# MLP up products of four groups as seven block products, with weight sums made in DRAM by timed DMAs

## The chip, the cores and the metric

The kernel runs on one core of a Trainium2 chip. The metric is the device time of one execution in microseconds (us); the time of a kernel is the median of its runs. Five engines each work through their own list of instructions: TensorE (PE) multiplies, VectorE (DVE), ScalarE (ACT) and GpSimd (POOL) do the elementwise work, SyncE (SP) issues transfers (DMAs). POOL issues transfers too. Semaphores order one engine's work behind another's.

## The reference

One layer on a sequence of 512 frames with 1024 features: a mixer (forgetting attention beside a gated recurrence), cross attention to 256 memory frames, and an MLP, each added to the residual, then a last norm. The change lies in the MLP (d_ff is 4096):

```python
u = rmsnorm(h, norm_ff_g[l]) @ w1[l]
h = h + jnp.square(jax.nn.relu(u)) @ w2[l]
return rmsnorm(h, final_norm_g)
```

All is float32. The kernel splits each operand into a high and a low part and computes a product as three matmuls: high by high, high by low, low by high.

## The kernel before, in words

The program is written out by hand; each engine works in program order, apart from places where a filler (`fill`) puts projections between the steps of the attention. Up to about 430 us it does the mixer and the cross attention. Weights come through SP in pieces of 512 KB into raw tiles (`wr`), ACT makes the high part (`wh`, L175) and DVE the low part (`wl`, L179).

The MLP works in eight groups of 512 hidden features. **Up**: for each of two halves `j` of the group and each of two blocks `i` of 128 features, a PSUM bank `u` takes 8 x 3 matmuls of 512 columns (`mlp_up`, `gemm_fm`, L240 to L242; weights stationary, x moving as `x_hi` and `x_lo`). ACT makes the squared ReLU in two steps (`square`, L1306 and L1307). **Down**: each group's product is a 2 by 2 block product (rows of frames by halves of features) in seven products instead of eight, after Strassen and Winograd (`mlp_down`, `PLAN`): `hidden_sums` combines the hidden blocks, `hidden_part` splits a combination into `hb`, and seven combined weight blocks are multiplied with them in banks U, V and Y. DVE adds a bank to the accumulator `acc` after the products that complete it, scaled by the norm's factor `rsq` (`add_to`, L1334). Up of group g+1 comes before down of group g; the last two groups' downs are done together, and `last_product` ends the program.

The combined weight blocks of the down are made in the SBUF: SP loads five raw blocks of w2 per group into eight slots (`load_raws`, tiles `wq`), and four accumulating transfers, issued by POOL (`add_weights`, L1244), add one block to another: two from DRAM (`first_adds`), two from slot to slot. The up's units are `wru`, `whu`, `wlu`; the down's `wq`, `whd`, `wld`. `unit` keeps four split units ahead of PE.

In the mixer, the biases of the forgetting attention (`bi`, L926 and L927) are made on POOL, for pairs of heads and one to four blocks of 128 keys, and DVE adds them to the scores (L946).

Of the kernel before, what the change touches and what calls it, by code (L numbers as in the profile page):

```python
# [38 lines left out]
NEG = -3.0e38  # L39


@with_exitstack
def emit(
# [189 lines left out]
    def gemm_fm(ps, wt, col, ahi, alo, n=S, order=range(KC), begun=False):  # L233

        whi, wlo = wt
        sl = slice(col, col + P)
        for n_, k in enumerate(order):
            hi, lo = chunk(ahi, k, slice(0, n)), chunk(alo, k, slice(0, n))
            wh, wl = chunk(whi, k, sl), chunk(wlo, k, sl)
            te.matmul(ps, wh, hi, start=n_ == 0 and not begun, stop=False)  # L240
            te.matmul(ps, wh, lo, start=False, stop=False)  # L241
            te.matmul(ps, wl, hi, start=False, stop=k == order[-1])  # L242
            yield 3 * n / 2400

    def gemm_tm(ps, wt, ahi, alo, tb, nk=KC):
# [3 lines left out]
        for k in range(nk):  # L249
# [5 lines left out]
            te.matmul(ps, lo, wh, start=False, stop=k == nk - 1)  # L255
            yield 3 * n / 2400

    def gemm_wide(pss, ahi, alo, done):

        for half in range(2):  # L260
            whi, wlo = next_panel()
            for u in range(2):
                for tb, ps in enumerate(pss):
                    sl = slice(tb * P, (tb + 1) * P)
                    for kk in range(2):
# [4 lines left out]
                        te.matmul(ps, lo, whi[u][:, kk, :], start=False, stop=k == KC - 1)  # L270
                        yield 3 * S / 2400
# [127 lines left out]
    xTd = drp.tile([4, P, 2, S], F32, name="xTd")  # L399
    park = {}  # L400
# [817 lines left out]
    slots = [t[:, i, :] for t in [ap_.tile([P, 4, D], F32, tag="act", name=f"wq{j}") for j in range(2)] for i in range(4)]  # L1218
    HS = S // 2
    units, raws, unit_q = {}, {}, deque()  # L1220
    sqs, comb, hbs = {}, {}, {}

    def up_units(g):
        for j in range(2):
            spec = panel(w1, g * HG + j * WT)
            for n in range(2):

                def prep(g=g, j=j, n=n, spec=spec):
                    if (j, n) == (0, 0):
                        down_raws(g - 1)  # L1230
                    unit, splits = load_unit(f"u{g}{j}{n}", spec, slice(n * UK, (n + 1) * UK))
                    with ahead(PW):
                        for split in splits:
                            split()
                    units["u", g, j, n] = unit

                unit_q.append((("u", g, j, n), prep))

    quad = {"a1": (0, 0), "c1": (0, 0), "a2": (0, 1), "b2": (1, 1), "b1": (1, 0)}
    PRODUCTS = ("1", "2", "6", "5", "7", "3", "4")  # L1240

    def add_weights(raw, src):

        gp.dma_start(raw.rearrange("p (k n) -> p k n", k=2), src, accum_op=ALU.add)  # L1244

    RAWS = ("a1", "c1", "a2", "b2", "b1")

    def load_raws(g, names):
        w = raws.setdefault(g, {})
        for name in names:  # L1250
            r, c = quad[name]
            n = 5 * g + RAWS.index(name)
            w[name] = slots[n % 8] if n < 38 else k4([D], f"wq{n}")
            src = w2[g * HG + r * 2 * P : g * HG + (r + 1) * 2 * P, c * S : (c + 1) * S].rearrange("(k p) n -> p k n", p=P)
            nc.sync.dma_start(w[name].rearrange("p (k n) -> p k n", k=2), src)
            w[name, "src"] = src

    def first_adds(g):
        w = raws[g]
        add_weights(w["a2"], w["b2", "src"])  # L1260
        add_weights(w["c1"], w["a2", "src"])

    def down_raws(g):

        load_raws(g, RAWS)
        first_adds(g)


    RAW = {"1": "a1", "2": "b1", "5": "c1", "3": "b2", "6": "a1", "7": "a2", "4": "b1"}

    def down_units(gs):
        def prep(g, name):
            w = raws[g]
            raw = w[RAW[name]]
            unit = new_parts([2, S], f"d{g}{name}")
            with ahead(PW):
                split_of(unit[0], unit[1], raw.rearrange("p (k n) -> p k n", k=2))()
            if name == "2":
                for to, of in (("a1", "a2"), ("b1", "a1")):
                    add_weights(w[to], w[of].rearrange("p (k n) -> p k n", k=2))  # L1280
            units["d", g, name] = unit

        for name in PRODUCTS:
            for g in gs:
                unit_q.append((("d", g, name), lambda g=g, name=name: prep(g, name)))
# [9 lines left out]

    def mlp_up(g, j, wt):
        for i in range(2):
            ps = mm(f"u{g}{j}{i}")
            run_now(gemm_fm(ps, wt, i * P, x2_hi, x2_lo))
            yield g, j, i, ps  # L1300

    def square(g, j, i, ps):
        if i == 0:
            sqs[g, j] = k4([2, S], f"sq{g}{j}")
        u = sqs[g, j][:, i, :]
        ac.activation(u, ps, AF.Relu)  # L1306
        ac.activation(u, u, AF.Square)  # L1307

    def hidden_sums(g):
# [7 lines left out]
        comb[g] = {"1": A1a, "5": s5, "6": n6, "3": s3, "7": s7, "2": A1b, "4": A2b}  # L1317

# [11 lines left out]

    def add_to(ps, rows, half, t, sign):
        tb = 2 * rows + t
        a = acc[tb][:, half * S : (half + 1) * S]
        ve.scalar_tensor_tensor(a, ps, rsq[sign][:, tb : tb + 1], a, op0=ALU.mult, op1=ALU.add)  # L1334


    PLAN = {
        "1": ("U", True, ((0, 0, 1),)),
# [4 lines left out]
        "2": ("V", True, ((0, 0, 1),)),  # L1343
# [3 lines left out]
    def mlp_down(gs):  # L1347
# [3 lines left out]
        for n, name in enumerate(PRODUCTS):  # L1351
# [4 lines left out]
            for g, t in [(g, t) for g in gs for t in range(2)]:  # L1356
                whi, wlo = unit("d", g, name)
                hb = hbs[g, name]
                if first_ and g == gs[0]:
                    banks[bank, t] = {"U": sc, "Y": tr, "V": mm}[bank](f"{bank}{g}{t}")  # L1360
# [193 lines left out]
```

## Time and profile before

| | us |
|---|---|
| Three runs | 766.42, 766.53, 766.06 |
| Median | 766.42 |
| Profiled execution | 766.06 |
| Its span (first to last instruction) | 764.3 |
| PE busy | 755.3 |
| DVE busy | 502.8 |
| ACT busy | 388.6 |
| POOL busy | 170.3 |

The span holds everything that the profile shows; 1.7 us of the execution lie outside it. Busy times of different engines overlap. A row of matmuls gives how long one is in flight, and several are at once: the pace is the distance between start times. A row of a transfer gives the time from its issue to its landing. A row of a group reads: line, engine, operation, output and input, count, then busy time and the mean in ns, then the idle time of the engine ahead of it and what ended that.

### The profile page before, as it was taken

The page shows a single profiled execution, that of the slowest core. Times are in us where ns is not written, and L with a number is a line of the kernel's source. Part 1 is how long each engine was busy: PE and PEld are TensorE (multiplying, and loading weights), DVE is VectorE, ACT ScalarE, POOL GpSimd, SP SyncE. Part 2 cuts the span into 40 slices and gives each one's busy share as a digit, 9 for nine tenths or more (in the row PEclk, how much of TensorE's full clock was granted, in tenths as well). Part 3 has the DMA queues.
Part 4 walks back from the last instruction along what each step waited for, and adds up shares of the span by engine and source line. Part 5 has one row for each costly group of instructions (what it writes and reads, how often), then busy time and mean ns, then how long its engine had stood idle before and what let it go on. Part 6 is the DMA issues. An engine that isn't in the chain of part 4 may idle for free.

```text
span 764.3 us, 10886 instructions
## 1 busy us (share of the span) xinstructions
PE 755.3 (99%) x4069; PEld 635.5 (83%) x4069; DVE 502.8 (66%) x816; ACT 388.6 (51%) x657; POOL 170.3 (22%) x248
## 2 busy tenths in 40 slices
PE   9999999999999999999999999999999999999996
PEld 6889888888889988888888888888888888888885
DVE  5647863678877656555546445939495776767596
ACT  6655554656666523344444456455454545353653
POOL 7207531322542225310000110101001010101123
PEclk9999999999999999999999999999999999999999
DMA  8652333313635432222113595575758575758602
GB/s 241 201 138 58 85 84 111 111 56 111 197 111 172 138 129 83 84 98 67 56 56 103 204 280 129 153 171 160 179 156 198 143 189 142 193 138 217 141 1 110
DMA packets 78870, 103.01 MB, mean 135 GB/s; under 512 B 4657, under 2 KB 56410, under 8 KB 78818
## 3 DMA queue, kind: packets, MB, share of 16 engines
q1 hardware_dynamic: 69266, 76.61, 32.1%
q0 software_dynamic: 8960, 24.67, 15.5%
q10 hardware_dynamic: 592, 1.05, 0.4%
q8 instruction: 32, 0.52, 0.3%
q14 instruction: 20, 0.16, 0.1%
HBM read 89.71 MB, written 4.21 MB: 123 GB/s over the span
## 4 chain that ended last, share of the span: by engine, by line
PE 95%; DVE 2%; ACT 1%; POOL 1%; issue 1%; ACTq 0%; POOLq 0%
PE u L240 8%; PE u L241 8%; PE u L242 8%; PE U L1366 4%; PE U L1367 4%; PE U L1368 4%; PE xq L240 2%; PE wo L240 2%; PE xq L241 2%; PE xq L242 2%; PE xw L241 2%; PE xw L242 2%; PE wo L242 2%; PE xw L240 2%; PE wo L241 2%; PE Y L1366 2%
## 5 line engine op out<-in xcount | busy, mean ns | idle before, releaser
L179 DVE TENSOR_TENSOR wld<-wq,whd 128x1024 fp32r<-128x1024 f32 x56 | 68.8, 1240 | 46.8 <-ACT whd L175 46.8
L240 PE MATMUL u<-x_hi,whu 128*128 128x512 f32 x192 | 74.7, 389 | 0.0
L241 PE MATMUL u<-x_lo,whu 128*128 128x512 f32 x192 | 74.7, 389 | 0.0
L242 PE MATMUL u<-x_hi,wlu 128*128 128x512 f32 x192 | 74.7, 389 | 0.0
L175 ACT ACTIVATE whd<-wq 128x1024 fp32r<-128x1024 f32 x56 | 58.3, 1052 | 29.7 <-PE u L241 18.5
L1244 POOL DMA_DIRECT2D wq<-in_w_dram x16 | 19.4, 1228 | 178.4 <-DMA wq<-in_w_dram 124.7
L175 ACT ACTIVATE whu<-wru 128x1024 fp32r<-128x1024 f32 x24 | 25.3, 1053 | 56.9 <-DMA wru<-in_w_dram 56.9
L179 DVE TENSOR_TENSOR wlu<-wru,whu 128x1024 fp32r<-128x1024 f32 x24 | 29.3, 1222 | 33.0 <-ACT whu L175 33.0
L1366 PE MATMUL U<-whd,hb 128*128 128x512 f32 x120 | 46.7, 389 | 0.0
L1367 PE MATMUL U<-wld,hb 128*128 128x512 f32 x120 | 46.7, 389 | 0.0
L1368 PE MATMUL U<-whd,hb 128*128 128x512 f32 x120 | 46.7, 389 | 0.0
L242 PEld LDWEIGHTS u<-x_hi,wlu 128*128 128x128 f32 x192 | 36.0, 188 | 7.5
L240 PEld LDWEIGHTS u<-x_hi,whu 128*128 128x128 f32 x192 | 36.0, 188 | 7.5
L241 PEld LDWEIGHTS u<-x_lo,whu 128*128 128x128 f32 x192 | 36.0, 188 | 7.4
L1244 POOL DMA_DIRECT2D wq<-wq x16 | 14.1, 880 | 125.0 <-DVE wld L179 95.6
L1334 DVE SCALAR_TENSOR_TENSOR acc<-U,rsq,acc 128x512 f32<-128x512 f32 x56 | 39.8, 744 | 0.3 <-PE U L1393 0.3
L926 POOL TENSOR_SCALAR bi<-nF,Ft 128x128 f32<-128x128 f32 (+3 forms) x32 | 23.0, 726 | 58.0 <-PE pt L958 37.0
L1306 ACT ACTIVATE sq<-u 128x512 f32<-128x512 f32 x32 | 18.7, 584 | 20.5 <-PE u L242 20.5
L1368 PEld LDWEIGHTS U<-whd,hb 128*128 128x128 f32 x120 | 22.5, 188 | 4.7
L1366 PEld LDWEIGHTS U<-whd,hb 128*128 128x128 f32 x120 | 22.5, 188 | 4.7
L1367 PEld LDWEIGHTS U<-wld,hb 128*128 128x128 f32 x120 | 22.5, 188 | 4.7
L1324 ACT ACTIVATE hb<-s 128x512 fp32r<-128x512 f32 x24 | 15.0, 629 | 20.6 <-PE U L1368 13.6
(957 smaller groups left out, 2262.1 us busy)
## 6 DMA issues: line engine op xcount, KB each, us to landing
wq<-in_w_dram SPq DMA_DIRECT2D x40, 512.0 KB, 3.4
wru<-in_w_dram SPq DMA_DIRECT2D x24, 512.0 KB, 6.4
wq<-in_w_dram POOLq DMA_DIRECT2D x16, 512.0 KB, 8.7
wq<-wq POOLq DMA_DIRECT2D x16, 512.0 KB, 4.9
xTd<-xT POOLq DMA_DIRECT2D x4, 512.0 KB, 4.1
nF<-Fd POOLq DMA_DIRECT2D x8, 256.0 KB, 3.9
hT<-xTd POOLq DMA_DIRECT2D x4, 512.0 KB, 5.3
xt<-in_x_dram SPq DMA_DIRECT2D x3, 512.0 KB
```

The lines of the kernel that those rows point to most:

```text
L175: ac.activation(hi, raw, AF.Copy)
L179: ve.tensor_tensor(lo, raw, f(hi), ALU.subtract)
L240: te.matmul(ps, wh, hi, start=n_ == 0 and not begun, stop=False)
L241: te.matmul(ps, wh, lo, start=False, stop=False)
L242: te.matmul(ps, wl, hi, start=False, stop=k == order[-1])
L926: gp.tensor_scalar(bi[:, 0:n], fF[h][:, 0:n], -1.0, Ft[:, tb, h : h + 1], op0=ALU.mult, op1=ALU.add)
L1244: gp.dma_start(raw.rearrange("p (k n) -> p k n", k=2), src, accum_op=ALU.add)
L1306: ac.activation(u, ps, AF.Relu)
L1334: ve.scalar_tensor_tensor(a, ps, rsq[sign][:, tb : tb + 1], a, op0=ALU.mult, op1=ALU.add)
L1366: te.matmul(ps, hi, whi[:, k, :], start=begin, stop=False, skip_group_check=True)
L1367: te.matmul(ps, hi, wlo[:, k, :], start=False, stop=False, skip_group_check=True)
L1368: te.matmul(ps, lo, whi[:, k, :], start=False, stop=k == 1, skip_group_check=True)
```

## The change

**Up.** For groups 4 to 7 (`SEVEN`) the up is a block product in seven products too (`mlp_up7`). The four quarters of a group's weights (512 inputs by 256 features) and of x (512 inputs by 256 frames) are combined; each product has 4 x 2 x 3 matmuls of 256 columns. The combinations of x are made once, during the up of group 1 (`x_sums`). Products go to three banks: "1" to U, "5" to Y, "6" adds to U, "2" goes to V, "7" adds to U, "3" to Y, "4" to U. ACT copies U to V after "1" and to Y after "6", and Y after "5" to the tile `y5`, which DVE adds to two results (the sign is turned in the square's step).

**Weight sums.** For each group's down, and for the ups of groups 4 to 7, the four combined weight blocks are made in DRAM (`sum_jobs`, tiles `wsd` and `wsu`): eight transfers each, four copies (L427) and four accumulates (L425), all issued by POOL. A class `Presum` counts matmul time (2400 columns a us) as the program is written; after 80 us, and then after each 5 us, the next transfer is made to wait for the matmul just written. Jobs alternate in pairs. SP then loads raw and combined blocks alike (L1290) into a ring of five raw tiles. The accumulates and the slots in the SBUF go; the slots' room holds the combinations of x.

**Down.** The products' order becomes "1", "5", "6", "2", "7", "3", "4". "1" isn't added to `acc` any more: ACT copies its U into V (L1489), where "2" adds to it, so DVE does 12 adds a group, not 14. `acc` is scaled once by mean square + eps before the first down, so the adds need no factor, and the last norm's eps is scaled alike (`eps3`). `hidden_ahead` makes the hidden parts up to four products ahead.

The diff, cut:

```diff
+SEVEN = (4, 5, 6, 7)
+RAWS, HB = 5, 4
+PRE0, PRE = 80.0, 5.0
...
-            te.matmul(ps, wl, hi, start=False, stop=k == order[-1])
-            yield 3 * n / 2400
+            at = te.matmul(ps, wl, hi, start=False, stop=k == order[-1])
+            yield presum.tick(3 * n / 2400, at)
...
+    SUMS = {"5": ("00", "01"), "7": ("01", "11"), "6": ("5", "11"), "4": ("6", "10")}
+
+    def block1(g, rc):
+        r, c = int(rc[0]), int(rc[1])
+        n0 = g * HG + c * WT
+        return w1[r * S : (r + 1) * S, n0 : n0 + WT].rearrange("(k p) n -> p k n", p=P)
+
+    def block2(g, rc):
+        r, c = int(rc[0]), int(rc[1])
+        k0 = g * HG + r * 2 * P
+        return w2[k0 : k0 + 2 * P, c * S : (c + 1) * S].rearrange("(k p) n -> p k n", p=P)
+
+    wsum = {}
+
+    def sum_jobs(kind, g):
+        block, shape = (block1, [P, UK, WT]) if kind == "u" else (block2, [P, 2, S])
+        for name in SUMS:
+            wsum[kind, g, name] = drp.tile(shape, F32, name=f"ws{kind}{g}{name}")
+        for name, add in (("5", 0), ("7", 0), ("5", 1), ("7", 1), ("6", 0), ("6", 1), ("4", 0), ("4", 1)):
+            dst, (a, b) = wsum[kind, g, name], SUMS[name]
+            if add:
+                yield gp.dma_start(dst, block(g, b), accum_op=ALU.add)
+            else:
+                yield gp.dma_start(dst, wsum[kind, g, a] if a in SUMS else block(g, a))
+
+    class Presum:
+        def __init__(self):
+            self.jobs, self.left = deque(), PRE0
+
+        def tick(self, us, at):
+            self.left -= us
+            while self.left <= 0.0 and self.jobs:
+                job = self.jobs[0]
+                dma = next(job, None)
+                if dma is None:
+                    self.jobs.popleft()
+                    continue
+                sync = mybir.DependencyInfo(mybir.DependencyClass.Sync, mybir.DependencyReason.DATA)
+                tc.add_manual_dep(dma.ins, at.ins.name, sync, reason="presum")
+                if len(self.jobs) > 1:
+                    self.jobs[0], self.jobs[1] = self.jobs[1], self.jobs[0]
+                self.left += PRE
+            return us
+
+    presum = Presum()
+    for g in range(DFF // HG):
+        presum.jobs.append(sum_jobs("d", g))
+        if g + 2 in SEVEN:
+            presum.jobs.append(sum_jobs("u", g + 2))
...
+    PRODUCTS = ("1", "5", "6", "2", "7", "3", "4")
+    QUAD = {"1": "00", "2": "10", "3": "11"}
+    raw_n = [0]
+
+    def raw_tile(name):
+        raw_n[0] += 1
+        if raw_n[0] % RAWS in (0, 2):
+            return wrp.tile([P, D], F32, tag="wr", name=f"wr{name}", padded_shape=[P, UK * UW])
+        return s4([D], f"wr{name}")
+
+    def add_unit(key, shape, src):
+
+        def prep():
+            name = "".join(map(str, key))
+            unit = new_parts(shape, name)
+            raw = raw_tile(name).rearrange("p (k n) -> p k n", k=shape[0])
+            nc.sync.dma_start(raw, src())
+            with ahead(PW):
+                split_of(unit[0], unit[1], raw)()
+            units[key] = unit
+
+        unit_q.append((key, prep))
 
     def up_units(g):
+        if g in SEVEN:
+            for name in PRODUCTS:
+                add_unit(("u", g, name), [UK, WT], lambda name=name: block1(g, QUAD[name]) if name in QUAD else wsum["u", g, name])
+            return
         for j in range(2):
...
+                add_unit(("d", g, name), [2, S], lambda g=g, name=name: block2(g, QUAD[name]) if name in QUAD else wsum["d", g, name])
...
+    def mlp_up7(g):
+
+        qa, qb = (k4([2, S], f"sq{g}{j}") for j in range(2))
+        sqs[g, 0], sqs[g, 1] = qa, qb
+        h1, h2 = slice(0, HS), slice(HS, S)
+        bank = {}
+
+        for name in PRODUCTS:
+            b = {"5": "Y", "3": "Y", "2": "V"}.get(name, "U")
+            if b not in bank:
+                bank[b] = (pvt if b == "Y" else mm)(f"u{b}{g}").rearrange("p (i n) -> p i n", i=2)
+                if b == "V":
+                    pass
+            ps = bank[b]
+            whi, wlo = unit("u", g, name)
+            xh, xl = xsum[name]
+            for k in range(UK):
+                for i in range(2):
+                    ws, begin = slice(i * P, (i + 1) * P), name in "15" and k == 0 and i == 0
+                    te.matmul(ps[:, i, :], whi[:, k, ws], xh[:, k, :], start=begin, stop=False, skip_group_check=True)
+                    te.matmul(ps[:, i, :], whi[:, k, ws], xl[:, k, :], start=False, stop=False, skip_group_check=True)
+                    at = te.matmul(ps[:, i, :], wlo[:, k, ws], xh[:, k, :], start=False, stop=k == UK - 1, skip_group_check=True)
+                presum.tick(6 * HS / 2400, at)
+            if name == "1":
+                bank["V"] = mm(f"uV{g}").rearrange("p (i n) -> p i n", i=2)
+                ac.activation(bank["V"], ps, AF.Copy)
+            elif name == "5":
+                y5 = t2(f"y5{g}", F32, (2, HS))
+                ac.activation(y5, ps, AF.Copy)
+            elif name == "6":
+                ac.activation(bank["Y"], ps, AF.Copy)
+            elif name == "2":
+                square(ps, qa[:, :, h1])
+            elif name == "7":
+                ve.tensor_tensor(qb[:, :, h2], ps, y5, ALU.add)
+                square(qb[:, :, h2], qb[:, :, h2], -1.0)
+            elif name == "3":
+                ve.tensor_tensor(qb[:, :, h1], ps, y5, ALU.add)
+                square(qb[:, :, h1], qb[:, :, h1], -1.0)
+            else:
+                square(ps, qa[:, :, h2])
+            yield
...
+        for n, (a, b, sign) in (("5", ("4", "2a", -1)), ("6", (None, "1", 1)), ("3", (None, "2", -1)), ("7", ("1", "2a", -1))):
+            op = ALU.add if sign > 0 else ALU.subtract
+            if a is None:
+                ve.tensor_tensor(d, d, f(x_[b][0]), op)
+            else:
+                ve.tensor_tensor(d, f(x_[a][0]), f(x_[b][0]), op)
+                ve.tensor_tensor(d, d, f(x_[a][1]), ALU.add)
+            ve.tensor_tensor(d, d, f(x_[b][1]), op)
+            yield
+            hi, lo = out_[n]
+            ac.activation(hi, d, AF.Copy, scale=-1.0 if n == "6" else 1.0)
+            if n == "6":
+                ve.scalar_tensor_tensor(lo, d, -1.0, f(hi), op0=ALU.mult, op1=ALU.subtract)
+            else:
+                ve.tensor_tensor(lo, d, f(hi), ALU.subtract)
+            xsum[n] = (hi, lo)
+            yield
 
     def hidden_sums(g):
...
+    def hidden_ahead(key, n):
+
+        used = hb_order.index(key)
+        for k in hb_order[used : used + n]:
+            if k not in hbs and k[0] in comb:
+                hidden_part(*k)
...
-        ve.scalar_tensor_tensor(a, ps, rsq[sign][:, tb : tb + 1], a, op0=ALU.mult, op1=ALU.add)
-
+        a = acc[2 * rows + t][:, half * S : (half + 1) * S]
+        if sign > 0:
+            ve.tensor_tensor(a, ps, a, ALU.add)
+        else:
+            ve.scalar_tensor_tensor(a, ps, -1.0, a, op0=ALU.mult, op1=ALU.add)
...
             for g, t in [(g, t) for g in gs for t in range(2)]:
                 whi, wlo = unit("d", g, name)
+                hidden_ahead((g, name), 1)
...
-                if end and (g, t) == (gs[0], 1) and 1 <= n < len(PRODUCTS) - 1:
-                    hidden_part(NG - 1, PRODUCTS[n + 1])
-                for rows, half, sign in goes if g == gs[-1] else ():
+                    at = te.matmul(ps, lo, whi[:, k, :], start=False, stop=k == 1, skip_group_check=True)
+                presum.tick(6 * S / 2400, at)
+                if end and (g, t) == (gs[0], 1):
+                    hidden_ahead((g, name), HB + 1)
+                if g != gs[-1]:
+                    continue
+                if name == "1":
+                    banks["V", t] = mm(f"V{g}{t}")
+                    ac.activation(banks["V", t], ps, AF.Copy)
+                for rows, half, sign in goes:
                     add_to(ps, rows, half, t, sign)
                     if end and (name, rows) in FINAL:
                         finish(2 * rows + t, half)
-            if not end:
-                hidden_part(gs[0] + 1, name)
-            elif n == 0:
-                hidden_part(NG - 1, PRODUCTS[1])
+            hidden_ahead((gs[-1], name), HB)
+            yield
 
     def last_product(gs, banks):
...
+    e2 = cp.tile([P, NT], F32, name="e2")
+    eps3 = cp.tile([P, NT], F32, name="eps3")
...
+    gp.tensor_tensor(eps3, e2, e2, op=ALU.mult)
+    gp.tensor_scalar(eps3, eps3, EPS, 0.0, op0=ALU.mult, op1=ALU.add)
+    for tb in range(NT):
+        ac.activation(acc[tb], acc[tb], AF.Copy, scale=e2[:, tb : tb + 1])
```

**What moves on the engines.** First PE, in the fifth up (group 4). Before, a bank `u` ends after 24 matmuls of 512 columns, and the bank of the next 128 features begins, with the same weights unit:

```order
2854 L241 MATMUL u_5592<-x_lo,whu_5536 128x512
2855 L242 MATMUL u_5592<-x_hi,wlu_5537 128x512
2856 L240 MATMUL u_5620<-x_hi,whu_5513 128x512
2857 L241 MATMUL u_5620<-x_lo,whu_5513 128x512
2858 L242 MATMUL u_5620<-x_hi,wlu_5514 128x512
2859 L240 MATMUL u_5620<-x_hi,whu_5513 128x512
```

After, product "1" ends after 24 matmuls of 256 columns and "5" begins in the bank Y, with the combined x (`xs`):

```order
2854 L1353 MATMUL uU_5716<-x_lo,whu_5643 128x256
2855 L1354 MATMUL uU_5716<-x_hi,wlu_5644 128x256
2856 L1352 MATMUL uY_5749<-xs_hi,whu_5667 128x256 [waits Activation_49]
2857 L1353 MATMUL uY_5749<-xs_lo,whu_5667 128x256
2858 L1354 MATMUL uY_5749<-xs_hi,wlu_5668 128x256 [waits DVE_49]
2859 L1352 MATMUL uY_5749<-xs_hi,whu_5667 128x256
```

The number of matmuls until here is the same; a group's up takes 168 of 256 columns and not 96 of 512. Next ACT in the same up, before: two steps of a square for each bank, and splits of later units between them:

```order
463 L1306 ACTIVATE sq_5617<-u_5592 128x512 [waits PE_49]
464 L1307 ACTIVATE sq_5617<-sq_5617 128x512 [waits Activation_49]
465 L175 ACTIVATE whu_5582<-wru_5584 128x1024 [waits DMAHW1_49,DVE_49]
466 L175 ACTIVATE whd_5588<-wq_4461 128x1024 [waits DMAHW4_49,DVE_49,PE_49]
467 L175 ACTIVATE whd_5647<-wq_4460 128x1024 [waits DMAHW4_49,DVE_49,PE_49]
468 L1306 ACTIVATE sq_5617<-u_5620 128x512 [waits PE_49]
469 L1307 ACTIVATE sq_5617<-sq_5617 128x512 [waits Activation_49]
470 L1324 ACTIVATE hb_5740<-sq_5617 128x512 [waits Activation_49]
471 L1306 ACTIVATE sq_5682<-u_5657 128x512 [waits PE_49]
472 L1307 ACTIVATE sq_5682<-sq_5682 128x512 [waits Activation_49]
```

After, from the last split ahead of the copy of U into V:

```order
474 L178 ACTIVATE whu_5750<-wru_5752 128x1024 [waits DMAHW0_49,PE_49]
475 L1358 ACTIVATE uV_5747<-uU_5716 128x512 [waits PE_49]
476 L178 ACTIVATE whu_5783<-wru_5785 128x1024 [waits DMAHW1_49,PE_49]
477 L1361 ACTIVATE y_5781<-uY_5749 128x512 [waits PE_49]
478 L178 ACTIVATE whu_5814<-wru_5816 128x1024 [waits DMAHW2_49,DVE_49,PE_49]
479 L1363 ACTIVATE uY_5749<-uU_5716 128x512 [waits PE_49,Activation_49]
480 L1428 ACTIVATE hb_6004<-s_3_5537 128x512 [waits DVE_49]
481 L178 ACTIVATE whd_5847<-wrd_5849 128x1024 [waits DMAHW4_49,PE_49]
482 L1321 ACTIVATE sq_5714<-uV_5747 128x2x256 [waits PE_49]
483 L1322 ACTIVATE sq_5714<-sq_5714 128x2x256 [waits Activation_49]
```

Each copy that clears a bank stands behind one split; the squares come behind the third copy. Last POOL, in the mixer, where the biases for three blocks of keys (128x384) are made. Before:

```order
102 L926 TENSOR_SCALAR bi_1859<-nF_1583,Ft 128x384 [waits PE_49,Activation_49]
103 L926 TENSOR_SCALAR bi_1864<-nF_1585,Ft 128x384 [waits PE_49]
104 L927 AFFINE_SELECT bi_1859<-bi_1859 128x128 [waits Pool_49]
105 L927 AFFINE_SELECT bi_1864<-bi_1864 128x128 [waits Pool_49]
106 L926 TENSOR_SCALAR bi_1951<-nF_1583,Ft 128x512 [waits DVE_49,PE_49]
107 L926 TENSOR_SCALAR bi_1956<-nF_1585,Ft 128x512 [waits DVE_49,PE_49]
108 L927 AFFINE_SELECT bi_1951<-bi_1951 128x128 [waits Pool_49]
109 L927 AFFINE_SELECT bi_1956<-bi_1956 128x128 [waits Pool_49]
```

After:

```order
108 L425 DMA wsd_1266<-in_w_dram 256x1x512 [waits DMASW1_49,DMASW0_49,PE_49]
109 L425 DMA wsd_1311<-in_w_dram 256x1x512 [waits DMASW3_49,PE_49]
110 L979 TENSOR_SCALAR bi_1875<-nF_1596,Ft 128x384 [waits Activation_49]
111 L979 TENSOR_SCALAR bi_1880<-nF_1598,Ft 128x384
112 L980 AFFINE_SELECT bi_1875<-bi_1875 128x128 [waits Pool_49]
113 L980 AFFINE_SELECT bi_1880<-bi_1880 128x128 [waits Pool_49]
114 L427 DMA wsd_1267<-wsd_1265 16x8192 [waits DMASW6_49,DMASW2_49,PE_49]
115 L979 TENSOR_SCALAR bi_1968<-nF_1596,Ft 128x512 [waits DVE_49,PE_49]
116 L979 TENSOR_SCALAR bi_1973<-nF_1598,Ft 128x512 [waits DVE_49,PE_49]
117 L980 AFFINE_SELECT bi_1968<-bi_1968 128x128 [waits Pool_49]
```

Two accumulates that wait for a matmul (`PE`) now stand ahead of these biases, and a copy that waits for another ahead of the next.

158 lines of the change are left out of this document (62 added, 96 removed).

## The prediction

> **What bounds the kernel now.** I read the page first: the span, the busy times and the chain.
>
> ```profile
> span 764.3 us, 10886 instructions
> PE 755.3 (99%) x4069; PEld 635.5 (83%) x4069; DVE 502.8 (66%) x816; ACT 388.6 (51%) x657; POOL 170.3 (22%) x248
> PE 95%; DVE 2%; ACT 1%; POOL 1%; issue 1%; ACTq 0%; POOLq 0%
> ```
>
> PE is busy for 755.3 of 764.3 us, and 95% of the chain is its own. So two things only can move the end: less matmul time, or a wait of PE that is not there today. The view of waits, for PE, shows how little of the second there is:
>
> ```profile
> PE warm L352 <- DVE ones L356: 1.3, 1, 1.3
> PE pt L958 <- DVE bi L950: 0.7, 1, 0.7
> ```
>
> That is 2.0 us in the program and none of it in the MLP, which is where most of the change lies. The busy time by stages, for one up (first row) and one down product (second row) of the MLP, shows how far the others are from their limit there (columns: window, its length, then busy of PE, PEld, DVE, ACT, POOL with counts, the granted clock, the DMA engines' share, GB/s):
>
> ```profile
> 492.90:514.60 21.70, 21.70 (x98) 17.96 (x97) 11.13 (x13) 9.18 (x12) 2.97 (x3) 1.00 0.75 174
> 514.60:533.70 19.10, 19.10 (x86) 15.83 (x85) 17.66 (x24) 10.73 (x14) 1.21 (x1) 1.00 0.55 162
> ```
>
> PE fills both windows at the full clock. DVE is at 92% of the down window (17.66 of 19.10) and half idle in the up window; the DMA engines are at 0.75 and 0.55. These are the covers that the change spends.
>
> **The change part by part. 1. Matmuls.** An up group has 2 x 2 x 8 x 3 = 96 matmuls of 512 columns. Seven products on quarter blocks are 7 x 4 x 2 x 3 = 168 matmuls of 256 columns. The pace of each is read from the start times of matmuls that follow each other: 14 steps of the up product, and 21 steps of the memory keys' product, which has the same form as the new ones (weights stationary, 256 columns moving, x as hi and lo).
>
> ```profile
> 499.79 0.39 PE L242 MATMUL u<-x_hi,wlu 128*128 128x512 f32 x1
> ...
> 502.96 0.39 PE L241 MATMUL u<-x_lo,whu 128*128 128x512 f32 x1
> ```
> ```profile
> 246.33 0.28 PE L240 MATMUL xk<-meh,wh19a 128*128 128x256 f32 x1
> ...
> 248.85 0.28 PE L240 MATMUL xk<-meh,wh19a 128*128 128x256 f32 x1
> ```
>
> 3.17/14 = 0.2264 us and 2.52/21 = 0.120 us: half the columns cost 53%, not 50%. A group falls from 96 x 0.2264 = 21.7 us to 168 x 0.120 = 20.2 us: 1.6 us (21.73 less 20.16), and 6.3 us over four groups. One eighth of the products is saved, 2.7 us, and two fifths of that goes to the shorter matmuls' dearer columns. The down products keep their 84 matmuls.
>
> The Trainium skill, "TensorE: Matmul & The Clock Gate", section "Back-to-back issue gap", gives the isolated gap as N/2.4 + 2.5 ns, by which I estimate 109 and 216 ns, a gain of 2.4 us a group and of 9.5 us in all. The measured 120 and 226 ns are longer than both; the sum goes by them.
>
> **2. DMA.** This decides whether the gain arrives. Prices come from the page's queue table and the landing times of its issues:
>
> ```profile
> q1 hardware_dynamic: 69266, 76.61, 32.1%
> q0 software_dynamic: 8960, 24.67, 15.5%
> wq<-in_w_dram SPq DMA_DIRECT2D x40, 512.0 KB, 3.4
> wru<-in_w_dram SPq DMA_DIRECT2D x24, 512.0 KB, 6.4
> wq<-in_w_dram POOLq DMA_DIRECT2D x16, 512.0 KB, 8.7
> wq<-wq POOLq DMA_DIRECT2D x16, 512.0 KB, 4.9
> xTd<-xT POOLq DMA_DIRECT2D x4, 512.0 KB, 4.1
> nF<-Fd POOLq DMA_DIRECT2D x8, 256.0 KB, 3.9
> hT<-xTd POOLq DMA_DIRECT2D x4, 512.0 KB, 5.3
> ```
>
> q1 takes 0.321 x 764.3 = 245 us of all 16 engines for 76.61 MB, so a load of 512 KB (0.524 MB) takes 1.68 us. q0 takes 118.5 us; its plain transfers (xTd, hT, nF, and mt and gfin, 7.9 MB) at q1's rate take 25.3 us, which leaves 93.2 us for 32 accumulates, 2.91 us each. These prices give the stage rows back: an up and a down hold 9 loads and 4 accumulates, 9 x 1.68 + 4 x 2.91 = 26.8 us, and the rows say 0.75 x 21.7 + 0.55 x 19.1 = 26.8.
>
> After the change, an up and a down of groups 4 to 7 last 20.2 + 19.0 = 39.2 us and need 14 loads, seven a stage, 23.5 us. The sums in DRAM come every 5 us of matmul time, counted at 2400 columns a us (168 x 256 + 84 x 512 columns are 35.84 us): 7.17 DMAs a pair, half copies and half accumulates, 3.58 x (1.68 + 2.91) = 16.4 us. Together 39.9 us of 39.2: **102% of the engines**, where the earlier pairs come to 11 x 1.68 + 3.84 x (1.68 + 2.91) = 36.1 of 40.8 us (88%). The pairs that still hold sums are about 3.3, since the last of the 96 falls in the last up. What is over is at most 0.8 x 3.3 = 2.5 us. Between the matmul that frees a load's buffer and the load's first use there stand at least 13 us of matmuls, against 6.4 us of landing, so some is absorbed: I take 1.3 us, between 0 and 2.5. SP's loads of sums also wait for the accumulate that ends the sum; those of the last two groups come last, begun until the third product of the last up, and the latest of them feeds the last product of the program, some 40 us of matmuls later: 0.
>
> No row shows a copy or an accumulate whose target is DRAM. The nearest: xT goes out to DRAM (xTd) in 4.1 us and comes back in 5.3, so a target in DRAM has no surcharge there; but an accumulate that reads DRAM lands in 8.7 us and one within the SBUF in 4.9. I bound a copy and an accumulate together by 3.4 us (both as cheap as a load) and 7.5 us (a copy at 1.68 and an accumulate at twice 2.91, about what 8.7 is to 4.9); I take 4.6, the two rows' own price, since they hold the same work with another target. Before 440 us there is room; the sums start at about 111 us, and two windows there say so (same columns as above):
>
> ```profile
> 320.00:360.00 40.00, 40.00 (x214) 34.37 (x213) 21.14 (x39) 17.80 (x35) 2.40 (x3) 1.00 0.21 67
> 440.00:480.00 40.00, 40.00 (x178) 33.14 (x177) 21.14 (x28) 24.02 (x37) 4.37 (x5) 1.00 0.80 204
> ```
>
> **3. Gates on POOL.** Each of the 96 DMAs waits on POOL for a matmul, and the FoX biases stand behind it on that queue. The tightest place that I find in the order is the first pair of three-block biases, now behind the eighth gate:
>
> ```profile
> 154.77 1.58 POOL L926 TENSOR_SCALAR bi<-nF,Ft 128x384 f32<-128x384 f32 x2
> 156.31 0.55 POOL L927 TENSOR_SCALAR_AFFINE_SELECT bi<-bi 128x128 f32<-128x128 f32 x2
> 162.63 0.28 PE L255 MATMUL fv<-wh11a,hn_lo 128*128 128x256 f32 x1
> 171.50 0.56 DVE L946 CUSTOM_DVE_ANT_0 bi<-ps,bi 128x384 f32<-128x384 f32 x1 [0.47 <-PE ps L936]
> L1244 POOL DMA_DIRECT2D wq<-in_w_dram x16 | 19.4, 1228 | 178.4 <-DMA wq<-in_w_dram 124.7
> ```
>
> The eighth gate, counted along the matmuls, is the row at 162.63. With an issue of 1.2 us, the biases are made from 164.1 on and ready at 166.3, 9.4 us later than now; DVE takes them at 171.50. 5.2 us are left: cost 0. Without this cover each us of delay is a us of PE.
>
> **4. DVE and ACT.** Seven splits replace four in the up of a group, three copies leave banks, and the down loses two of 14 adds:
>
> ```profile
> L179 DVE TENSOR_TENSOR wld<-wq,whd 128x1024 fp32r<-128x1024 f32 x56 | 68.8, 1240 | 46.8 <-ACT whd L175 46.8
> L175 ACT ACTIVATE whd<-wq 128x1024 fp32r<-128x1024 f32 x56 | 58.3, 1052 | 29.7 <-PE u L241 18.5
> L1334 DVE SCALAR_TENSOR_TENSOR acc<-U,rsq,acc 128x512 f32<-128x512 f32 x56 | 39.8, 744 | 0.3 <-PE U L1393 0.3
> L1306 ACT ACTIVATE sq<-u 128x512 f32<-128x512 f32 x32 | 18.7, 584 | 20.5 <-PE u L242 20.5
> L1328 DVE TENSOR_TENSOR hb<-sq,hb 128x512 fp32r<-128x512 f32 x24 | 16.5, 687 | 1.7 <-ACT hb L1324 1.7
> ```
>
> DVE in a pair: 14 x 1.24 + 12 x 0.744 + (7 lo parts + 4 hidden sums) x 0.687 + 2 x 0.744 = 35.3 us of 39.2. ACT: 14 x 1.05 + 5 copies and 8 square steps at about 0.6 + 7 hi parts at 0.63 = 26.9. Both fit: 0. The added work of the start (x's sums during the second up, four scalings of acc ahead of the first down) is 14 times 1.24 on DVE, 8 times 1.05 us on ACT, falls where the row of 440 to 480 us leaves DVE 18.9 and ACT 16.0 us idle, and x's sums are not used before the fifth up, 100 us on: 0.
>
> One handoff is tight. In the new up, U is written by "1", then "5" goes to Y, then "6" writes U again. "5" is 24 x 0.120 = 2.88 us, in which ACT must copy U away, behind a split that may just have begun: 1.05 + 0.58 = 1.6, and some 0.2 for the signal. 1.1 us are left, three times a group: 0.
>
> **Sum.** 6.3 less 1.3 is 5.0 us. The profiled execution took 766.06 us (span 764.3, 1.7 outside): 761.1. The median of the three runs is 766.42, 0.36 more; I forecast it at **761.4**. No change is told from a change within 0.2%, 1.5 us: 764.9 to 768.0.
>
> **The rivals.** *A, the forecast*: 766.42 - 6.3 = 760.1 with no loss, 762.6 with the whole 2.5. The scores of the cross attention step faster, also at 256 columns, and would give 1 us more:
>
> ```profile
> 360.05 0.28 PE L1128 MATMUL xs<-kT,xqh 128*128 128x256 f32 x1
> ...
> 360.88 0.28 PE L1129 MATMUL xs<-kT,xql 128*128 128x256 f32 x1
> ```
>
> 0.83/7 = 0.1186 us, 19.9 us a group, 758.8 without a loss. So 758.8 to 762.6. Chance 0.58.
>
> *B, slower: the DMA engines saturate in groups 4 to 7.* For it: 102% at my own prices, and the two prices that matter are of transfers that the trace lacks; accumulates from DRAM land later than the others. Against it: PE waits for no load at 0.80 now, and writing to DRAM showed no surcharge. With a copy and an accumulate at p together, the loss is 3.3 x (23.5 + 3.58 p - 39.2). It eats the 6.3 us at p = 4.9 and makes the kernel slower by over 1.5 us from p = 5.05 on, 10% above mine: 768. At p = 5.4 it is 772, and at the bound of 7.5 at least 797, where the earlier pairs overflow too. Chance 0.26. The PE would show waits for the weights' splits, behind late loads.
>
> The Trainium skill, "DMA: Bandwidth & Descriptors", section "Latency and other measured facts", gives copies between HBM tensors about 207 to 214 GB/s per direction, an estimate of 2.5 us for 512 KB; and its section "Issuing engines are not separate DMA queues" has all queues interleave on the same 16 engines. By that a copy and an accumulate cost 5.4 us and the time is about 772. No run here shows such a copy.
>
> *C, the handoffs*: a split and a hidden part more ahead of each copy cost 1.05 + 0.63 us where 1.1 are left: 0.6 us at 12 handoffs, 7 us: 767.1, no change. For it: DVE and ACT are fuller than now. Against: the order has one split there. Chance 0.08.
>
> *D, late biases*: gates that fall several us later than counted, behind an earlier DMA's own waits, make PE wait between 111 and 310 us: 2 to 6 us off the gain, 763 to 766. Against: 5.2 us of cover. Chance 0.05.
>
> *E*: 256 columns in exactly half the time of 512, a gain of 2.7 us a group (21.73/8): 755.6. Against: 0.120. Chance 0.03. The Trainium skill's gap formula, named above, comes near to it.
>
> **How the numbers follow.** Faster by over 0.2%: A, E and half of D, 0.63. The same: half of D and most of C, 0.09. Slower: B and the rest of C, 0.28. The range goes from A's low end, 758.8, through C and D, into B as far as 772, p at 0.8 us or 17% above the price I take, where about half of B's chance is used up: outside lie E and the rest of B, some 0.16.
>
> **What would show it.** The up of groups 4 to 7 in 20.2 us, steps of 0.120 us; PE's waits there under 3 us in all, none from 111 to 310; the DMA share near 0.9 to 1.0 in the pairs, with loads landing in under 13 us; DVE at some 90% of a pair. I am wrong if PE waits for splits behind loads (B, with the accumulates' landing well above 8.7 us), for uV, uY or y5 (C), or for bi (D).

## The result, and the profile after

The median of 20 runs is 766.37 us, and of 20 runs of the kernel before 766.4: a ratio of 1.0 (95% interval 0.9986 to 1.0014). No change, where 761.4 was forecast. The runs of the changed kernel lie far apart, from 761.7 to 772.0 us; those of the kernel before lie between 766.0 and 767.9. The profiled execution took 769.98 us and so shows a bad case, 3.6 us over the median.

The page of the changed kernel, with the lines that answer to those of before:

```profile
span 768.3 us, 11718 instructions
PE 752.7 (98%) x4357; PEld 646.2 (84%) x4357; DVE 526.3 (69%) x834; ACT 420.8 (55%) x703; POOL 220.1 (29%) x314
q1 hardware_dynamic: 69714, 91.29, 36.4%
q0 software_dynamic: 23680, 58.22, 34.2%
PE 91%; DMA 5%; DVE 1%; issue 1%; ACT 1%; ACTq 0%; DVEq 0%; SPq 0%
```

The chain had no DMA before; now 5% of it is DMA. PE's waits, 2.0 us before, are 9.0:

```profile
PE uU L1352 <- ACT uV L1358: 4.3, 1, 4.3
PE pt L1011 <- DVE dn L1002: 1.7, 1, 1.7
PE warm L355 <- DVE ones L359: 1.3, 1, 1.3
PE uU L1352 <- ACT uY L1363: 1.2, 1, 1.2
PE u L245 <- DVE wlu L182: 0.5, 1, 0.5
```

The stages of the fifth to seventh up, and of the down behind the fifth (second row; columns as in the prediction), show both halves of the story:

```profile
578.14:598.30 20.16, 20.16 (x170) 20.15 (x169) 14.22 (x16) 13.66 (x19) 2.78 (x3) 1.00 1.06 326
598.30:617.36 19.06, 19.06 (x86) 15.78 (x85) 17.40 (x23) 11.70 (x15) 3.30 (x4) 1.00 0.89 246
617.36:638.95 21.59, 20.41 (x169) 20.20 (x168) 14.22 (x16) 13.81 (x19) 2.31 (x4) 1.00 0.97 321
658.02:684.20 26.18, 21.89 (x170) 21.69 (x169) 14.60 (x16) 13.85 (x19) 3.05 (x4) 0.93 0.83 260
```

The fifth up takes 20.16 us, to the hundredth what 168 x 0.120 gives, at a DMA share of 1.06: the share adds the times of the packets, so it can pass 1, and a share of 1 is no limit at which PE stops. The sixth up loses 1.4 us and the seventh 6.0. The chain of waits of the seventh, in order of time (start, length, what), and ACT's own row where the load lands:

```profile
652.77 12.29 DMA wru<-in_w_dram
665.25 0.87 issue
666.12 0.61 ACT hb L1428
666.74 0.95 ACT whu L178
667.68 0.49 ACT uV L1358
668.22 0.39 PE uU L1352
```
```profile
665.16 1.06 ACT L178 ACTIVATE whu<-wru 128x1024 fp32r<-128x1024 f32 x1 [8.60 <-DMA wru<-in_w_dram]
```

A load of raw weights takes 12.3 us to land. ACT stands idle for 8.6 us ahead of its split, and behind that in ACT's queue stand a hidden part, one more split and the copy of U into V, for which PE waits. PE does not need those weights yet: it is about to begin "6", and they are those of "2", the next product. One stall lies before the MLP, of the same kind: a panel's load, its split on ACT, and behind it a block of the forgetting attention (`bi`, `dn`):

```profile
229.42 6.84 DMA wr19a<-in_w_xkv_dram
236.29 1.07 ACT wh19a L178
...
240.42 1.22 PE pt L1011 x8
```

After the long wait PE's clock fell too. Windows of 2 us, and the pace inside (256 columns in 0.21 us, before and after that in 0.12):

```profile
668.00:670.00 2.00, 1.78 (x11) 1.78 (x12) 1.54 (x2) 0.88 (x2) 0.00 (x0) 0.76 1.07 280
670.00:672.00 2.00, 2.00 (x12) 2.00 (x11) 1.23 (x1) 0.83 (x2) 0.53 (x1) 0.50 1.02 385
672.00:674.00 2.00, 2.00 (x17) 2.00 (x17) 0.14 (x1) 1.23 (x2) 0.00 (x0) 0.88 1.11 424
670.07 0.41 PE L1354 MATMUL uU<-xs_hi,wlu 128*128 128x256 f32 x1
670.28 0.41 PE L1352 MATMUL uU<-xs_hi,whu 128*128 128x256 f32 x1
```

The clock missing in these windows is 2 x (0.24 + 0.50 + 0.12) = 1.7 us. So the 4.3 us of the wait cost 6.0, which is what the stage lost. For this execution: 766.06 - 6.3 + 7.0 of new waits + 1.7 of clock = 768.5, of 769.98. The rest is not in this view of waits: the third up, for one, lasts 22.7 us (21.8 before), of which it has 0.5.

### The profile page after: what moved, and what is told of

Same layout as the page of the kernel before. It is cut to its first block, busy times and chain, and to the rows that moved or that the text cites. A ratio compares the mean times of both kernels' runs of the same rounds, so it can differ in the third digit from the quotient of the medians.

```text
span 768.3 us, 11718 instructions
## 1 busy us (share of the span) xinstructions
PE 752.7 (98%) x4357; PEld 646.2 (84%) x4357; DVE 526.3 (69%) x834; ACT 420.8 (55%) x703; POOL 220.1 (29%) x314
## 3 DMA queue, kind: packets, MB, share of 16 engines
q1 hardware_dynamic: 69714, 91.29, 36.4%
## 4 chain that ended last, share of the span: by engine, by line
PE 91%; DMA 5%; DVE 1%; issue 1%; ACT 1%; ACTq 0%; DVEq 0%; SPq 0%
PE u L245 4%; PE u L243 4%; PE u L244 4%; PE U L1479 3%; PE U L1480 3%; PE U L1481 3%; DMA wru<-in_w_dram 3%; PE xq L243 2%; PE wo L243 2%; PE xq L244 2%; PE xw L243 2%; PE xq L245 2%; PE xw L245 2%; PE xw L244 2%; PE wo L244 2%; PE wo L245 2%
## 5 line engine op out<-in xcount | busy, mean ns | idle before, releaser
L182 DVE TENSOR_TENSOR wld<-wrd,whd 128x1024 fp32r<-128x1024 f32 x56 | 68.4, 1221 | 32.2 <-ACT whd L178 32.2
L178 ACT ACTIVATE whd<-wrd 128x1024 fp32r<-128x1024 f32 x56 | 59.0, 1056 | 30.5 <-PE u L244 9.7
L425 POOL DMA_DIRECT2D wsd<-in_w_dram x32 | 34.4, 1076 | 121.1 <-PE Y L1481 24.7
L425 POOL DMA_DIRECT2D wsu<-in_w_dram x16 | 18.9, 1181 | 64.9 <-PE u L245 13.6
L427 POOL DMA_DIRECT2D wsd<-in_w_dram x16 | 10.9, 682 | 62.8 <-PE uU L1354 20.3
L1001 ACT ACTIVATE bi<-bi,mx 128x128 f32<-128x128 f32 (+3 forms) x32 | 17.9, 559 | 16.5 <-DVE mx L999 16.5
L245 PE MATMUL u<-x_hi,wlu 128*128 128x512 f32 x64 | 25.0, 391 | 0.5 <-DVE wlu L182 0.5
L243 PE MATMUL u<-x_hi,whu 128*128 128x512 f32 x64 | 25.0, 391 | 0.0
L244 PE MATMUL u<-x_lo,whu 128*128 128x512 f32 x64 | 24.9, 389 | 0.0
L1479 PE MATMUL Y<-whd,hb 128*128 128x512 f32 x64 | 24.9, 389 | 0.0
L1480 PE MATMUL Y<-wld,hb 128*128 128x512 f32 x64 | 24.9, 389 | 0.0
L1481 PE MATMUL Y<-whd,hb 128*128 128x512 f32 x64 | 24.9, 389 | 0.0
```

Source lines behind the costliest of these rows:

```text
L178: ac.activation(hi, raw, AF.Copy)
L182: ve.tensor_tensor(lo, raw, f(hi), ALU.subtract)
L245: at = te.matmul(ps, wl, hi, start=False, stop=k == order[-1])
L425: yield gp.dma_start(dst, block(g, b), accum_op=ALU.add)
L1001: ac.activation(b, b, AF.Exp, bias=mx, scale=-1.0, accum_out=den)
L1479: te.matmul(ps, hi, whi[:, k, :], start=begin, stop=False, skip_group_check=True)
```

## The experiments

The theory after the result: the DMA engines are full where sums and loads meet, some loads land after 10 us and more, and ACT, which works in order, passes the delay on to PE (theory 1). The rival: the handoffs of banks are late by themselves, since ACT and DVE have more to do (theory 2). Each ratio below is to the kernel before, run beside it.

**No sums.** The 96 transfers go, and SP loads a raw block in place of each sum.

```diff
-    for g in range(DFF // HG):
-        presum.jobs.append(sum_jobs("d", g))
...
-add_unit(("u", g, name), [UK, WT], lambda name=name: block1(g, QUAD[name]) if name in QUAD else wsum["u", g, name])
+add_unit(("u", g, name), [UK, WT], lambda name=name: block1(g, QUAD[name]) if name in QUAD else block1(g, SUB[name]))
```

> Leaves out all 96 copies and accumulates that make weight sums in DRAM; SP loads a plain block of the weights in place of each sum, so the products are of wrong blocks. Seven-product ups, loads, splits and handoffs stay. Theory 1 (the DMA engines are full, loads land late, ACT's queue stands behind a late load): 766.4 - 6.4 = 760.0 us within 0.5, all runs within 1 us of each other, PE waits about 2 us in all, clock 0.999. Theory 2 (the handoffs of banks are late by themselves, since ACT and DVE are fuller): stays at 765 to 767 with the spread, and PE still waits for uV and uY.

Measured: 760.16 us (759.69 to 760.91), ratio 0.9918 (0.9906 to 0.993). PE's waits are those of before to a tenth, and loads land in 3.4 and 4.2 us, against 7.2 and 6.3 in the changed kernel (last two rows):

```profile
PE warm L355 <- DVE ones L359: 1.3, 1, 1.3
PE pt L1008 <- DVE bi L1000: 0.7, 1, 0.7
wrd<-in_w_dram SPq DMA_DIRECT2D x56, 512.0 KB, 3.4
wru<-in_w_dram SPq DMA_DIRECT2D x36, 512.0 KB, 4.2
q0 software_dynamic: 2304, 7.89, 3.1%
```
```profile
wrd<-in_w_dram SPq DMA_DIRECT2D x24, 512.0 KB, 7.2
wru<-in_w_dram SPq DMA_DIRECT2D x20, 512.0 KB, 6.3
```

The matmuls' gain is 6.3 us, and the new handoffs cost nothing by themselves: theory 2 falls.

**Copies only.** Each accumulate becomes a plain copy.

```diff
-                yield gp.dma_start(dst, block(g, b), accum_op=ALU.add)
+                yield gp.dma_start(dst, block(g, b))
```

> Each of the 48 accumulates is a plain copy to the same place (the sums are not made). Same 96 transfers, same waits on POOL, same loads. Theory 1 with the accumulate's price as the cause: a pair of groups 4 to 7 needs 14 x 1.6 + 7.17 x 1.6 = 33.9 us of the engines in 39.2 (86%), where now it is 14 x 1.6 + 3.58 x 4.95 = 40.1: 760 to 762 us, spread under 2 us. If the number of transfers or the gates on POOL are the cause and not the engines' time: 765 to 768 as now.

Measured: 759.81 us (759.31 to 759.91), ratio 0.9911 (0.9898 to 0.9924). As many transfers and gates on POOL as in the changed kernel cost nothing; so the accumulates are what costs. PE's waits beside the first (`warm`) fall to 0.2 us. The prices follow from the queues:

```profile
PE pt L1011 <- DVE bi L1003: 0.2, 1, 0.2
q0 software_dynamic: 13440, 58.22, 22.8%
```

Without sums q0 takes 0.031 x 758.5 = 23.5 us. 0.228 x 758.2 = 172.9 us less that, over 96, is 1.56 us a copy within DRAM: cheaper than the 1.68 of a load before. In the changed kernel 0.342 x 768.3 = 262.8 us, less 23.5 and 48 copies (74.9), leaves 3.43 us for an accumulate, where 2.91 was forecast. A load in the changed kernel takes 1.61 us (0.364 x 768.3 = 279.7 us for 91.29 MB).

**Half the accumulates.** Those of sums "6" and "4" become copies, by one more `if` at the same place.

> Half the accumulates (those of sums 6 and 4) are plain copies, so these sums are wrong; 24 accumulates stay. A copy and an accumulate cost 1.55 and 3.45 us, so a pair of groups 4 to 7 needs 14 x 1.6 + 5.38 x 1.55 + 1.79 x 3.45 = 36.9 us of 39.2 (94%). If the engines' time is the cause: 760 to 762 us, spread 1 to 3 us. If each accumulate makes its own stall: half way, about 763.

Measured: 760.96 us (760.26 to 762.88), ratio 0.9929 (0.9917 to 0.9942). The 24 that stay cost 1.2 us beside no accumulates (760.96 - 759.81) and not half of the 6.6 us that 48 cost (766.37 - 759.81): the cost does not come in equal parts with each accumulate, but where they crowd. The longer of the two waits that its profile adds in the MLP (1.8 and 0.5 us) is the known one, and its chain begins with a load of 9.8 us:

```profile
PE uU L1355 <- ACT uV L1361: 1.8, 1, 1.8
649.10 9.77 DMA wru<-in_w_dram
```

**No seven-product ups**, all 96 transfers kept.

```diff
-SEVEN = (4, 5, 6, 7)
+SEVEN = ()
-        if g + 2 in SEVEN:
+        if g + 2 in (4, 5, 6, 7):
```

> Ups of groups 4 to 7 as four plain units and 96 matmuls of 512 columns again; all 96 transfers for sums stay, also those that nobody reads now. Theory 1: PE gains nothing and a pair needs 11 x 1.6 + 3.84 x 4.95 = 36.6 us of 40.8 (90%), so the early stalls stay (2.1 us before the MLP, about 1 us in groups 0 to 3): 767.5 to 770, with a spread of some us. Theory 2 (handoffs of the new up): 766.4 within 0.5, spread as before.

Measured: 767.62 us (766.79 to 770.48), ratio 1.0021 (1.0011 to 1.003). The first up begins at 432.2 us, 2.4 later than without sums (429.8), and from there PE needs 327.6 us to its end, as before the change. In the MLP, with 11 loads a pair, 90% full by the new prices (11 x 1.61 + 3.84 x 4.99 = 36.9 of 40.8), no load is late enough. So the losses are of two sorts, one before the MLP from the sums alone, one in the MLP, most of it in groups 4 to 7, where sums meet 14 loads a pair.

**ACT in written order** in the new ups (`manual_schedule` around the body of `mlp_up7`).

> In the ups of groups 4 to 7 ACT works in the order in which the code is written: the copy of U into V stands ahead of the split of the fifth product's weights, not behind it, and so on for each copy; nothing else is changed. Theory 1 with ACT's queue as the link (a late load blocks a copy that does not need it): PE's waits for uV and uY nearly go, 762.5 to 764.5 us. If late loads stop PE just as well through the weights themselves: 765.5 to 767.

Measured: 771.11 us (767.78 to 774.15), ratio 1.0058 (1.0039 to 1.0078): slower, which neither side had expected. The order that it made also moves hidden parts and squares, and its profile shows short waits for splits all over the downs (`Y` for `wld` 1.4 us, for `whd` 1.1). It doesn't tell the two apart, and why it lost was not followed further. The next one makes the same edit alone.

**Copy first.** The next split on ACT is made to depend on the copy that clears a bank; nothing else moves.

```diff
-                ac.activation(bank["V"], ps, AF.Copy)
+                hold[0] = ac.activation(bank["V"], ps, AF.Copy)
...
+                tc.add_manual_dep(last_hi[0].ins, hold[0].ins.name, sync, reason="hold")
```

> In the ups of groups 4 to 7 each copy that clears a bank (uV, y5, uY) stands ahead of the next split on ACT, by a dependency of that split on the copy; all else, and ACT's other order, stays as in the changed kernel. If ACT's queue behind a late load is what turns late loads into PE's waits there: 763.5 to 765 (the 2 us before the MLP stay, the waits for uV and uY go). If a late load stops PE anyway, a little later: 765.5 to 767.5.

Measured: 764.61 us (762.73 to 765.32), ratio 0.997 (0.9958 to 0.9982). That is faster than the kernel before. Beside the changed kernel, 1.8 us off the median of five runs is not clear of noise: nine of the 20 runs of the changed kernel lie below 764.61. The profile tells more. In the seventh up the load for product "2" is late again, and the copy now follows ahead of the next split:

```profile
660.51 1.06 ACT L180 ACTIVATE whu<-wru 128x1024 fp32r<-128x1024 f32 x1 [6.16 <-DMA wru<-in_w_dram]
662.00 0.58 ACT L1364 ACTIVATE uV<-uU 128x512 f32<-128x512 f32 x1
662.60 1.06 ACT L180 ACTIVATE whu<-wru 128x1024 fp32r<-128x1024 f32 x1
PE uU L1358 <- ACT uV L1364: 0.9, 1, 0.9
```

The first split begins 4.7 us after this up (655.81). With half the accumulates and the changed kernel's order, the same split begins 4.6 us after the up (658.97, the up at 654.34), so the load is as late, and PE waits 1.8 us. The 0.9 us between the two waits are the one split that now stands behind the copy (0.95 us in the changed kernel's chain). So ACT's order is shown to be a link from a late load to PE's wait, but this edit is worth one split only: the late load's own split stands ahead of the copy in both orders, and of the 4.3 us in the changed kernel's profile it would take about 1 (an estimate from these two waits). The longest load of this profile, 12.51 us, feeds a split behind all three copies, in both orders, and cost 0.6 us.

**Other times for the 96 transfers.** The step of `Presum` becomes a table (count up to which, us of matmul time).

```diff
-PRE0, PRE = 80.0, 5.0
+PRE0 = 80.0
+PACE = (16, 3.75), (23, 5.7), (29, 5.0), (63, 3.9), (99, 6.75)
```

> The same 96 transfers, only their times change: the step between them is 3.75 us of matmul time for the first 16, then 5.7 (7), 5.0 (6), 3.9 (34) and 6.75 for the rest, so that fewer fall where loads are dense (200 to 260 us, and the last four groups) and more where the engines idle (300 to 470 us). A pair of groups 4 to 7 then needs 14 x 1.6 + 2.65 x 5.0 = 35.7 of 39.2 us (91%, was 103%). If the engines' time is the cause: 760 to 762.5 us with a spread of 2 to 4 us. If any accumulate beside seven-product loads makes stalls, however they are paced: 765 to 767.

> As e5_paced, but begun after 50 us of matmul time and not 80, and thinner at the end: 3.75 (24), 5.7 (7), 5.0 (6), 3.9 (34), 7.2 (13), 9.3 (12). A pair of groups 4 to 7 needs 14 x 1.6 + 2 x 5.0 = 32.5 of 39.2 us (83%) at most 36. If the engines' time is the cause: 760 to 761.5, as without sums, unless the early waits on POOL delay the recurrence there, which would show as PE waits before 130 us.

Measured: 766.54 us (763.31 to 770.85) and 767.34 us (764.5 to 770.46), ratios 1.0005 (0.9988 to 1.0022) and 1.0008 (0.9994 to 1.0021). A miss for both, and an instructive one: in both profiles groups 4 to 7 run without any wait, each up in 20.15 us, and the loss has moved ahead of the MLP, whose first up begins at 437.2 and 435.3 us, against 429.8 without sums (the first run loses 1.3 us more in its first down). The chain of the first shows panel after panel:

```profile
230.38 7.24 DMA wr19a<-in_w_xkv_dram
250.51 8.60 DMA wr21b<-in_w_xkv_dram
269.81 8.12 DMA wr23b<-in_w_out_dram
```

From 200 to 290 us panels pass through two raw tiles, so a load is issued only when the split before it is done and has little time to land; a somewhat thinner row of sums there (5.7 in place of 5.0) did not save it. Why these two lose more here than the changed kernel is not shown: their DMA share from 200 to 290 us is 0.75 and 0.74, that of the changed kernel 0.78, and with half the accumulates 0.76 costs nothing. So in this stage the share alone does not tell the loss.

**A gap there, and an early start.** Steps of 3.75 us from 50 us of matmul time, none at all for 71 us (about 185 to 285 us of the span), then 3.6 and 6.3; first with the copy first, then without.

```diff
-PRE0, PRE = 80.0, 5.0
+PRE0 = 50.0
+PACE = (21, 3.75), (22, 71.0), (57, 3.6), (99, 6.3)
```

> Two changes together. Times of the 96 transfers: from 50 us of matmul time on every 3.75 us (21), then none for 71 us of matmul time (about 185 to 285 us, where the mixer's and the cross attention's panels are loaded through two raw tiles), then every 3.6 us (35) and 6.3 us to the end. And e7_copy_first's order on ACT. A pair of groups 4 to 7 needs 14 x 1.6 + 2.84 x 5.0 = 36.6 of 39.2 us (93%). If late loads behind dense transfers are the whole cause: no waits before the MLP beyond 1 us, 760 to 762 us, spread under 3 us. If stalls only move to where the transfers now stand (71 to 185 or 300 to 470 us): 764 to 767.

> The times of the transfers as in e9_gap_copy, ACT's order as in the changed kernel. Tells how much of e9_gap_copy is the order on ACT: with the engines at 93% I expect few late loads and so little from the order, 760.5 to 763.5; if the order is what counts, 1.5 us or more above e9_gap_copy.

Measured: 761.35 us (760.0 to 762.88) and 760.9 us (760.14 to 763.92), ratios 0.9938 (0.9926 to 0.995) and 0.9933 (0.992 to 0.9947). Both beat both kernels, by 5 us and more, and all sums are made. PE's waits with the gap alone, and the windows of the panels and of groups 4 to 7, in the changed kernel (first two rows) and with the gap (last two):

```profile
PE warm L356 <- DVE ones L360: 1.3, 1, 1.3
PE pt L1013 <- DVE bi L1005: 0.6, 1, 0.6
PE uU L1354 <- ACT uY L1365: 0.5, 1, 0.5
```
```profile
200.00:290.00 90.00, 88.35 (x600) 77.32 (x599) 63.29 (x133) 46.53 (x88) 41.95 (x63) 1.00 0.78 220
575.00:713.00 138.00, 132.53 (x853) 121.69 (x852) 105.28 (x127) 83.30 (x110) 19.77 (x24) 0.99 0.92 275
```
```profile
200.00:290.00 90.00, 90.00 (x608) 78.95 (x607) 63.76 (x133) 47.91 (x89) 32.48 (x52) 1.00 0.46 147
575.00:713.00 138.00, 137.49 (x920) 127.32 (x919) 108.36 (x129) 88.43 (x118) 16.48 (x20) 1.00 0.87 264
```

A share of 0.87 in the MLP costs 0.5 us of PE, one of 0.92 cost 5.5. Each is one execution: the first took 760.14 us, the second 769.98. In the same window the other runs that keep ACT's order lose nothing up to a share of 0.84, and 1.8 and 0 us at 0.85 and 0.88. With loads in time, the order on ACT is worth nothing that these runs can tell (0.5 us between the two, the other way).

## Why the prediction was wrong

**Matmuls: right.** 20.16 us an up, 6.3 us over four; 760.1 without a loss was forecast, 760.16 measured without sums.

**DMA: wrong, and this is the step that failed.** The prediction took the loss from the mean: what is over 100% of the engines' time is "at most 0.8 x 3.3 = 2.5 us", of which it took 1.3, and nothing ahead of 440 us. The sums cost 6.2 us (766.37 with them, 760.16 without), through single late loads: in the changed kernel's profile one such load is behind 6.0 us, while the fifth up, at a share of 1.06, lost nothing.

The prices are not what failed. A copy and an accumulate cost 1.56 + 3.43 = 4.99 us, not 4.59: the copy had no surcharge, as xTd had suggested, and the accumulate was dearer than the mean of the two kinds that the kernel had; the sign of it, the landing of 8.7 against 4.9 us, went into the upper bound alone. But loads became cheaper, 1.61 us, so a pair needs 14 x 1.61 + 3.58 x 4.99 = 40.4 of 39.2 us, 103%, where 102% was forecast. With these prices the prediction's formula for B gives 3.3 x (40.4 - 39.2) = 4.0 us and 764.1, all of it in groups 4 to 7. With the old price of a load it gives 767.3, within 1 us of the result, and the line that a price of 4.9 eats the gain seems to come true; that is luck. B, with a chance of 0.26, was right that loads behind busy DMA engines stop PE, not in how much and where.

What it had wrong is, first, the cover. "At least 13 us" of matmuls stand between a load's issue and PE's use of its weights, and a load of 12.3 us is within that. With both parts of its split the weights were ready at 667.5 us, and PE, had nothing else stopped it, would have asked for them at about 666.7 (an estimate: three products of 2.88 us after 658.02): some 0.8 us of wait. But on ACT a bank's copy stands behind that split and is due a product sooner, and so PE stood for 4.3 us. The handoff had been priced with a split that "may just have begun", not with one that waits for its load.

Second, "before 440 us there is room" was read from a window of 40 us in the cross attention (320 to 360). 200 to 290 us, where panels use two raw tiles, was not priced; the sums cost 2.0 us ahead of the MLP in the changed kernel (its first up begins at 431.8 us) and 2.4 without seven-product ups.

**Gates on POOL: right.** With 96 gates and no accumulates PE waits less than before, and rival D falls. The late `bi` and `dn` in the chain above came from a load through ACT.

**DVE and ACT: right that both fit, wrong on what their queues hide.** The first new pair (578.14 to 617.36 us) takes 31.6 us of DVE and 25.4 of ACT, where 35.3 and 26.9 were forecast. C's price, a copy behind more than one split, never came by itself: without sums PE has no wait for a bank. The waits for uV and uY that were to mark C appeared, but as the sign of B.

**Not in the sum: the clock.** The three waits of 2.0 us and more that the profiles hold cost 1.7 us each beside themselves (the last section has them).

**The range** held the time; the chance of no change, 0.09, was too small. By the formula for B every price from 4.8 to 5.05 gives 764.9 to 768.0 us, no change, and no rival held these prices.

The Trainium skill, "DMA: Bandwidth & Descriptors", section "Latency and other measured facts", has its 207 to 214 GB/s for copies of 16 KiB rows on the sync and scalar queues. The estimate from it, 2.5 us for 512 KB, did not carry over to these copies: 1.56 us.

The Trainium skill, "Collectives: The Full Stack", section "The bandwidth ceiling: the fold count and why AG ≠ RS ≠ AR", says that in a ring the adding transfer (ReduceScatter) reads two sources on the same ring and so runs at half the rate of a copying one. The runs agree in size, 3.43 us for an accumulate against 1.56 for a copy, a factor of 2.2; the reason is not shown by them.

## What to carry to other kernels

Work moved to an idle engine's DMAs is paid from the same DMA engines as the loads: price it stage by stage, and ask not only whether the mean fits but which load has the fewest raw tiles behind it. Count a load's deadline to the first instruction in order behind its consumer, not to the matmul that uses it. When a transfer can be placed freely, leave it out of the stages with little buffering, even if they look half idle.

## What the runs showed of the hardware

PE's clock fell to half for about 3.4 us after waits of 4.3 us (changed kernel), 3.1 (early pace) and 2.0 us (first pace): the granted clock is 0.72 from 242 to 248 us in both paced runs, 1.7 us of clock missing in each. It did not fall after 1.9 (no seven-product ups), 1.8 (half the accumulates) or 1.7 (changed kernel, before the MLP). The rows of the shortest that did it:

```profile
241.77 1.38 PE L1013 MATMUL pt<-ident,bi 128*128 128x128 f32 x8 [2.05 <-DVE dn L1004]
...
244.44 0.41 PE L244 MATMUL xk<-meh,wh18a 128*128 128x256 f32 x1
244.65 0.41 PE L245 MATMUL xk<-mel,wh18a 128*128 128x256 f32 x1
```

The Trainium skill, "TensorE: Matmul & The Clock Gate", Part 1, puts the fall behind an idle window of about 3.4 us. Here 2.05 us of idle were enough once, while the slow stretch of about 3.4 us agrees with the length of its window.
